# Values and keys turned block-wise on VectorE and placed by GpSimd; 86 dense steps ahead of the corner; the inverses' round trip on GpSimd's queue

## The chip, the cores and the metric

The kernel runs on one core of a Trainium2 chip. The metric is the device time of one execution in microseconds (us). Engines are named as in the profile: PE (TensorE matmul), PEld (its weight loads), DVE (VectorE), ACT (ScalarE), POOL (GpSimd), SP (SyncE, which issues most DMAs).

## What is computed

One layer of a bidirectional mixer on 384 tokens (128 of context, 256 latent). A combined projection `h @ w_in` feeds a gated short convolution and an RWKV-7 scan with 32 heads of 64 channels, run forwards and backwards:

```python
def step(S, inp):
    r_t, w_t, k_t, v_t, a_t, b_t = inp
    sa = jnp.einsum('dbhij,dbhj->dbhi', S, a_t)
    S = S * w_t[..., None, :] + sa[..., :, None] * b_t[..., None, :] + v_t[..., :, None] * k_t[..., None, :]
    y = jnp.einsum('dbhij,dbhj->dbhi', S, r_t)
    return S, y
```

The branches are gated, projected (`w_out_a`, `w_out_b`), merged, projected by `w_o`, added to the input and normalised. The final scan states of the context are outputs too.

## The kernel before

**Dense stream.** All large projections run in fp32 as three matmuls of split operands (`mm3`, lines 81 to 83; `hi*hi`, `hi*lo`, `lo*hi`). The class `Stream` cuts them into steps: one step is three matmuls of 128x384 for one column block and one slice of the contraction. A pair of column blocks is 32 steps. Weights are loaded by SP (`raw`), split by ACT (`whi`, line 88) and DVE (`wlo`, line 89) four slices at a time. Pairs have tags: `rk` (r and k of a block), `gv` (gate of a block and v of the next), `bc`, `bx`, `bg`, `gb` (convolution branch), `ma`, `mb` (merge gates), `ob`, and last `oa`, which needs the finished branch A.

**Blocks.** The scan is done in 16 blocks of two heads (`b`), in chunks of 64 tokens (6 chunks, 2 directions). The loop at lines 961 to 990 writes dense steps between the pieces of a block's work, so PE's order is the order of the code. PE's order is fixed by hand; the order on DVE, ACT, POOL and SP is set by a scheduler from the same code. Per block:

- `prep_b`: the products `bk` (keys, 128 channels x 6 chunks x 128) and `pr`, 14 dense steps, then the triangular matrices `A` (PE line 703, masked by DVE line 709, direction by direction with 6 dense steps behind each). POOL scales `bk` by the chunk's decay (line 716). The diagonal 32x32 blocks of `A` go by DMA through DRAM (`ui`) into `U` (48 matrices, one per partition), DVE inverts them in 60 dependent instructions (lines 724 and 726), and the inverses go back by DMA (`uo`, line 729) into `A` (line 734). DVE then turns two of them into `x11` (line 737).
- `prep_c`: states are loaded; PE transposes v (`pv`, 6 transposes, into `sav`) and the scaled `bk` (`pb`, 10 transposes, into `bt`), ACT copies them out of PSUM.
- `prep_a` of the next block, once its `gv` pair is done, and dense steps until `WINDOW` = 80 of them have passed since `prep_b` (104 in block 0 with `FIRST`, 96 in block 15 with `LAST`).
- the corner in `scan`: `pav` (line 850, needs `sav`), `pH` (line 842, needs `x11`), `pX`, then two chains of `po`, `pq`, `pu` with dense steps between; POOL clears part of `A` (line 863).
- `norm`, and in the next block `finish`, which stores the block's part of branch A in DRAM (`ya_d`). After block 15 the rest of `ob` runs, `load_ya` loads all 16 parts back through three buffers (`yst_a`), and `oa` starts.

Of the kernel before, what the change touches and what calls it, by code (L numbers as in the profile page):

```python
# [21 lines left out]
C = 64  # L22
NCH = 6
# [33 lines left out]
def hybrid_step(ctx, tc, cst, x_prompt, x_sample, state_f, state_b, c, c_ctx, ada_w, ada_b, norm_g,  # L57
                w_in, mu_prev, mu_next, w0, w2, a0, a2, k_k, k_a, r_k, lnx_g, lnx_b, conv_w,
                w_out_a, w_out_b, w_o, final_g, y_prompt, y_sample, ns_f, ns_b):
    nc = tc.nc  # L60
# [30 lines left out]


    PB0, PB1, H0, H1, CH0, CH1 = 14, 6, 3, 4, 2, 4
    PRO, WINDOW, FIRST, LAST = 32, 80, 24, 16

    def wload(view, k0, cols, nm):

# [84 lines left out]
    ds_ = Stream()  # L182
# [226 lines left out]
    def tmp(nm):  # L409
        return box["sp"].tile([P, T], F32, tag="t", name=nm, bufs=8)  # L410
# [179 lines left out]
    def bank(nm):  # L590
        return ps1.tile([P, 4, P], F32, tag="A", name=nm, bufs=5)
# [4 lines left out]
    def flat(a):  # L596
        return a.rearrange("p n t -> p (n t)")
# [44 lines left out]
    def prep_k(b, o):  # L642
# [6 lines left out]
        for d in range(2):  # L649
# [14 lines left out]
            o["kd"].append(kd)  # L664
            o["bn"].append(aa)

    def prep_b(b, o):

        r, kk = r_[b], o["kk"]
# [27 lines left out]
        for d in range(2):  # L697
            pr, bk = o["pr"][d], o["bk"][d]
            m0 = C_MB if d else C_MF
            pas = {(h, n0): bank(f"pA_{b}_{d}_{h}_{n0}") for n0 in (0, 4) for h in range(2)}  # L700
            for n in range(NCH):
                for h in range(2):
                    TE.matmul(pas[h, n // 4 * 4][:, n % 4, :], bk[hss[h], n, :], pr[hss[h], n, :],  # L703
                              start=True, stop=True)
            for n0, w in ((0, 4), (4, 2)):
                mk = cs[:, m0:m0 + P].rearrange("p (w t) -> p w t", t=C).unsqueeze(1).broadcast_to([P, w, 2, C])
                for h in range(2):
                    f0 = NCH * d + n0
                    V.tensor_tensor(A[:, :, f0:f0 + w, hss[h]].rearrange("p w n t -> p n w t"),
                                    pas[h, n0][:, 0:w, :].rearrange("p n (w t) -> p n w t", t=C), mk, ALU.mult)  # L710
            yield PB1
            for e in range(2):
                nc.sync.dma_start(ui[d, e].rearrange("i s t -> s i t"), blocks(A, d, e))

        for d in range(2):
            G.tensor_tensor(o["bk"][d][:], o["bk"][d][:], o["ep"][d][:, :, C:C + 1].broadcast_to([P, NCH, P]), ALU.mult)

        U = sp.tile([48, 32, 32], F32, tag="U", name=f"U_{b}")
        nc.sync.dma_start(U[:], ui[:].rearrange("d e i s t -> (d e i) s t"))
# [6 lines left out]
            V.tensor_tensor(U[:, 0:s, s + 1:], U[:, 0:s, s + 1:], tv, ALU.add)  # L726
        dg = U[:].rearrange("p a b -> p (a b)")[:, 0:1024:33]
        V.tensor_scalar(dg, dg, 1.0, None, ALU.add)
        nc.sync.dma_start(uo[:].rearrange("d e i s t -> (d e i) s t"), U[:])
        x11 = sp.tile([64, 24, 32], F32, tag="x11", name=f"x11_{b}")  # L730
        o["x11"] = x11
        for e in range(2):
            for d in range(2):
                nc.sync.dma_start(blocks(A, d, e), uo[d, e].rearrange("i s t -> s i t"))

        for d in range(2):
            box["turned"] = V.transpose(x11[0:32, 12 * d:12 * d + 12, :], blocks(A, d, 0)).ins

    def prep_c(b, o):

        r, v, A = r_[b], v_[b], o["A"]

        s_in = sp.tile([P, 2, C], F32, tag="s_in", name=f"s_in_{b}")
        for d in range(2):
            for h in range(2):
                for jb in range(2):
                    p0 = C * h + 32 * jb
                    nc.sync.dma_start(s_in[p0:p0 + 32, d, :].rearrange("i (b j) -> i b j", j=32),
                                      ctx_st[d][0, 0, 2 * b + h].rearrange("(b i) j -> i b j", i=32)
                                      [:, :, 32 * jb:32 * jb + 32])  # L750

        sav = sp.tile([P, 2 * NCH, P], F32, tag="sav", name=f"sav_{b}")
        bt = sp.tile([P, 2 * NCH, P], F32, tag="bt", name=f"bt_{b}")
        o["sav"], o["bkt"] = sav, bt
        for d in range(2):
            if d == 0:
                src = v
            else:
                src = tmp(f"vr_{b}")
                S.copy(src[:], v[:, ::-1])  # L760
            pv = bank(f"pv_{b}_{d}")
            for q in range(3):
                TE.transpose(pv[:, q, :], src[:, q * P:(q + 1) * P], ident)
            for e in range(2):
                S.copy(sav[C:P, NCH * d + e:NCH * d + NCH:2, :], pv[C * e:C * e + C, 0:3, :])
            yield 1
        for d in range(2):

            for n0, n1 in (((0, 4), (4, 5)), ((0, 3), (4, 6)))[d]:
                pb = bank(f"pb_{b}_{d}_{n0}")  # L770
                for n in range(n0, n1):
                    TE.transpose(pb[:, n - n0, :], o["bk"][d][:, n, :], ident)
# [167 lines left out]
        V.tensor_tensor(ya[:], ya[:], ga_[b][:], ALU.mult)  # L940
        nc.sync.dma_start(ya_d[b], ya[:])

    def drive(gen, prio=0, at=None, fn=None):
        n = i = 0
        while True:
            if i == at:
                fn()
            i += 1
            with tc.high_priority(offset=prio):
                u = next(gen, None)  # L950
            if u is None:
                return n
            ds_.go(u)
            n += u
# [2 lines left out]
    cur = {}  # L957
    drive(prep_a(0, cur))
    prep_k(0, cur)
    prev = None  # L960
    for b in range(NB):
        if b < NB - 1:
            if b > 0:
                ds_.urgent += [(add_rk, b + 1), (add_gv, b)]
        if b == NB - 2:
            ds_.fills += [(add_gv, NB - 1)] + [(add_ob, g) for g in range(8)]
        pb_gen = prep_b(b, cur)
        ds_.go(next(pb_gen))
# [203 lines left out]
```

## Time and profile before

| | |
|---|---|
| runs | 2235.28, 2237.07, 2239.02 us (median 2237.07) |
| the profiled execution | 2234.36 us, span 2232.6 us |
| granted TensorE clock | 0.998 |
| PE, PEld, DVE, ACT, POOL busy | 2173.1, 2062.7, 1553.3, 1013.5, 115.7 us |
| DVE inversion, lines 724 and 726, 960 instructions | 309.3 us |
| POOL, line 716, 32 instructions | 49.3 us |
| ACT, copies out of `pv` and `pb`, lines 765 and 773 | 55.4 us |

PE is busy nearly throughout, so the time is PE's work plus the moments when its next instruction waits. Busy shares of the others matter only where such a wait ends on them. A matmul's recorded duration overlaps with the next one's; what it costs is read from the distance of the starts.

### The profile page before, as it was taken

What the parts mean: (1) busy time and instruction counts of PE and PEld (TensorE: products, weight loads), DVE (VectorE), ACT (ScalarE), POOL (GpSimd) and SP (SyncE); (2) the same over time, 40 slices, a digit from 0 to 9 for tenths busy, and PEclk for the clock granted to TensorE, in tenths of its full rate; (3) what the DMA queues carried; (4) which work ended last, traced back from release to release, by engine and by line L of the source; (5) the groups of instructions that cost most, each with busy time, mean ns of one, the idle gap of its engine ahead of it and who ended that gap; (6) DMA issues with size and microseconds to landing.
All of it is one profiled execution on the core that took longest, in us unless ns stands there. A gap on an engine that the chain in (4) does not pass through costs nothing.

```text
span 2232.6 us, 40518 instructions
## 1 busy us (share of the span) xinstructions
PE 2173.1 (97%) x16020; PEld 2062.7 (92%) x16020; DVE 1553.3 (70%) x3240; ACT 1013.5 (45%) x1784; POOL 115.7 (5%) x113
## 2 busy tenths in 40 slices
PE   5999999999999999999999999999999999999998
PEld 3589999999999999999999999999999999998988
DVE  3259567787878878777878787887777785444354
ACT  4245435454545454444445454546454633333333
POOL 2000000000000000000000000000000000000000
PEclk9999999999999999999999999999999999999999
DMA  9974454444343435343444434344445464886633
GB/s 338 346 211 128 131 141 116 116 117 118 108 132 107 130 100 131 106 130 100 121 108 127 112 107 133 107 122 126 124 118 139 144 196 143 294 281 233 220 132 113
DMA packets 426574, 335.25 MB, mean 150 GB/s; under 512 B 82496, under 2 KB 408720, under 8 KB 425488
## 3 DMA queue, kind: packets, MB, share of 16 engines
q1 hardware_dynamic: 424896, 330.91, 50.2%
q8 instruction: 126, 2.06, 0.4%
q10 hardware_dynamic: 432, 1.57, 0.2%
q14 instruction: 64, 0.52, 0.1%
q0 software_dynamic: 1056, 0.19, 0.1%
HBM read 305.80 MB, written 26.21 MB: 149 GB/s over the span
## 4 chain that ended last, share of the span: by engine, by line
PE 74%; DVE 12%; DMA 6%; ACT 4%; issue 2%; SPq 1%; POOL 0%; POOLq 0%; DVEq 0%; ACTq 0%
DMA raw_adah<-in_ada_w_dram 4%; PE d_rk L81 3%; PE d_rk L82 3%; PE d_rk L83 3%; PE d_gv L81 3%; PE d_gv L82 3%; PE d_gv L83 3%; PE d_oa L81 2%; PE pA L703 2%; PE d_oa L83 2%; PE d_oa L82 2%; PE d_mb L81 2%; PE d_mb L83 2%; PE d_mb L82 2%; PE d_bc L81 2%
## 5 line engine op out<-in xcount | busy, mean ns | idle before, releaser
L724 DVE TENSOR_TENSOR ut<-U 48x30 f32<-48x30 f32 (+14 forms) x480 | 154.8, 323 | 18.3 <-DMA U<-ui 5.5
L81 PE MATMUL d_rk<-h_hi,whi_rk 128*128 128x384 f32 x480 | 161.7, 337 | 0.6 <-ACT lst L554 0.6
L726 DVE TENSOR_TENSOR U<-U,ut 48x30 f32<-48x30 f32 (+14 forms) x480 | 154.5, 322 | 11.1
L81 PE MATMUL d_gv<-h_hi,whi_gv 128*128 128x384 f32 x480 | 160.6, 335 | 0.0
L82 PE MATMUL d_rk<-h_lo,whi_rk 128*128 128x384 f32 x480 | 160.5, 334 | 0.0
L83 PE MATMUL d_rk<-h_hi,wlo_rk 128*128 128x384 f32 x480 | 160.4, 334 | 0.0
L83 PE MATMUL d_gv<-h_hi,wlo_gv 128*128 128x384 f32 x480 | 160.4, 334 | 0.0
L82 PE MATMUL d_gv<-h_lo,whi_gv 128*128 128x384 f32 x480 | 160.4, 334 | 0.0
L88 ACT CAST whi_gv<-raw_gv 128x1024 fp32r<-128x1024 f32 (+1 forms) x64 | 64.0, 999 | 139.6 <-PE d_rk L82 100.0
L88 ACT CAST whi_rk<-raw_rk 128x1024 fp32r<-128x1024 f32 x60 | 63.0, 1054 | 110.8 <-PE d_rk L82 34.7
L89 DVE TENSOR_TENSOR wlo_rk<-raw_rk,whi_rk 128x1024 fp32r<-128x1024 f32 x60 | 72.9, 1218 | 45.3 <-ACT whi_rk L88 35.6
L81 PE MATMUL d_bc<-h_hi,whi_bc 128*128 128x384 f32 x256 | 92.2, 360 | 0.0
L81 PE MATMUL d_gb<-h_hi,whi_gb 128*128 128x384 f32 x256 | 92.2, 360 | 0.0
L81 PE MATMUL d_bg<-h_hi,whi_bg 128*128 128x384 f32 x256 | 92.2, 360 | 0.0
L81 PE MATMUL d_bx<-h_hi,whi_bx 128*128 128x384 f32 x256 | 92.1, 360 | 0.0
L81 PE MATMUL d_ma<-h_hi,whi_ma 128*128 128x384 f32 x256 | 91.6, 358 | 0.0
L81 PEld LDWEIGHTS d_rk<-h_hi,whi_rk 128*128 128x128 f32 x480 | 90.1, 188 | 0.9 <-ACT lst L554 0.9
L81 PE MATMUL d_mb<-h_hi,whi_mb 128*128 128x384 f32 x256 | 90.4, 353 | 0.0
L81 PEld LDWEIGHTS d_gv<-h_hi,whi_gv 128*128 128x128 f32 x480 | 90.1, 188 | 0.2
L81 PE MATMUL d_ob<-ybh,whi_ob 128*128 128x384 f32 x256 | 88.4, 345 | 2.0 <-DVE smb L521 1.0
L82 PEld LDWEIGHTS d_rk<-h_lo,whi_rk 128*128 128x128 f32 x480 | 90.2, 188 | 0.0
L82 PEld LDWEIGHTS d_gv<-h_lo,whi_gv 128*128 128x128 f32 x480 | 90.1, 188 | 0.0
(315 smaller groups left out, 6548.4 us busy)
## 6 DMA issues: line engine op xcount, KB each, us to landing
raw_adah<-in_ada_w_dram SPq DMA_DIRECT2D x64, 512.0 KB, 8.7
raw_rk<-in_w_in_dram SPq DMA_DIRECT2D x60, 512.0 KB, 5.3
raw_gv<-in_w_in_dram SPq DMA_DIRECT2D x60, 512.0 KB, 4.9
raw_ma<-in_w_in_dram SPq DMA_DIRECT2D x16, 1024.0 KB, 5.6
raw_mb<-in_w_in_dram SPq DMA_DIRECT2D x16, 1024.0 KB, 5.6
raw_bc<-in_w_in_dram SPq DMA_DIRECT2D x16, 1024.0 KB, 5.5
raw_bx<-in_w_in_dram SPq DMA_DIRECT2D x16, 1024.0 KB, 5.4
raw_bg<-in_w_in_dram SPq DMA_DIRECT2D x16, 1024.0 KB, 5.5
```

Of the source, the lines that this page charges most:

```text
L81: TE.matmul(out, wh, xh, start=start, stop=False)
L82: TE.matmul(out, wh, xl, start=False, stop=False)
L83: TE.matmul(out, wl, xh, start=False, stop=stop)
L88: S.copy(hi[0:rows], src)
L89: V.tensor_tensor(lo[0:rows], src, hi[0:rows].bitcast(F32), ALU.subtract)
L703: TE.matmul(pas[h, n // 4 * 4][:, n % 4, :], bk[hss[h], n, :], pr[hss[h], n, :], start=True, stop=True)
L724: V.tensor_tensor(tv, U[:, 0:s, s:s + 1].broadcast_to([48, s, w]), U[:, s:s + 1, s + 1:].broadcast_to([48, s, w]), ALU.mult)
L726: V.tensor_tensor(U[:, 0:s, s + 1:], U[:, 0:s, s + 1:], tv, ALU.add)
```

## The change

The 16 PE transposes of a block and their eight ACT copies are gone, and so is ACT's reversed copy of v. DVE turns `bk` in place in 32x32 blocks (two instructions of 128x768 a block) and v (two of 128x384, in the scan of the block before), and POOL moves the 32x32 blocks to their places: 32 copies into `bt`, 16 into `sav`, each of 32 partitions x 192. The store `uo` and the four loads into `A` are issued by POOL. `WINDOW` is 86, `FIRST` 18, `LAST` 10, so blocks 0 and 15 keep 104 and 96 steps; `prep_a` starts exactly 12 steps ahead of the corner.

```diff
-    PRO, WINDOW, FIRST, LAST = 32, 80, 24, 16
+    PRO, WINDOW, FIRST, LAST, PA = 32, 86, 18, 10, 12
...
+    def prep_v(b, o):
+        o["vt"] = []
+        for d in range(2):
+            x = sp.tile([P, T], F32, tag=f"vt{d}", name=f"vt_{b}_{d}")
+            V.transpose(x[:], v_[b][:, ::-1] if d else v_[b][:])
+            o["vt"].append(x)
...
+        with tc.issue_after(last):
+            for d in range(2):
+                V.transpose(flat(o["bk"][d][:]), flat(o["bk"][d][:]))
+        bt = sp.tile([P, 2 * NCH, P], F32, tag="bt", name=f"bt_{b}")
+        with tc.issue_after(lam):
+            for d, p, q in ((d, p, q) for d in range(2) for p in range(4) for q in range(4)):
+                put = G.tensor_copy(bt[32 * p:32 * p + 32, NCH * d:NCH * d + NCH, 32 * q:32 * q + 32],
+                                    o["bk"][d][32 * q:32 * q + 32, :, 32 * p:32 * p + 32]).ins
+        sav = sp.tile([P, 2 * NCH, P], F32, tag="sav", name=f"sav_{b}")
+        with tc.issue_after(put):
+            for d in range(2):
+                x = o["vt"][d][:].rearrange("p (n e t) -> p n e t", e=2, t=32)
+                for e in range(2):
+                    for q in range(4):
+                        G.tensor_copy(sav[C + 32 * e:C + 32 * e + 32, NCH * d:NCH * d + NCH, 32 * q:32 * q + 32],
+                                      x[32 * q:32 * q + 32, :, e, :])
...
-        nc.sync.dma_start(uo[:].rearrange("d e i s t -> (d e i) s t"), U[:])
+        G.dma_start(uo[:].rearrange("d e i s t -> (d e i) s t"), U[:])
...
-                nc.sync.dma_start(blocks(A, d, e), uo[d, e].rearrange("i s t -> s i t"))
+                G.dma_start(blocks(A, d, e), uo[d, e].rearrange("i s t -> s i t"))
...
-            pv = bank(f"pv_{b}_{d}")
-            for q in range(3):
-                TE.transpose(pv[:, q, :], src[:, q * P:(q + 1) * P], ident)
-            for e in range(2):
-                S.copy(sav[C:P, NCH * d + e:NCH * d + NCH:2, :], pv[C * e:C * e + C, 0:3, :])
-            yield 1
...
-                pb = bank(f"pb_{b}_{d}_{n0}")
-                for n in range(n0, n1):
-                    TE.transpose(pb[:, n - n0, :], o["bk"][d][:, n, :], ident)
-                S.copy(bt[:, NCH * d + n0:NCH * d + n1, :], pb[:, 0:n1 - n0, :])
-                yield 1
...
+        w = WINDOW + (FIRST if b == 0 else LAST if b == NB - 1 else 0)
         if b < NB - 1:
-            while f"gv{b}" not in ds_.done:
+            while n < w - PA or f"rk{b + 1}" not in ds_.done:
                 ds_.go(1)
                 n += 1
             n += drive(prep_a(b + 1, nxt))
```

What stands on POOL in block 7, before: the last instruction of block 6 (the root in `norm`), the scaling of `bk`, the clearing of `A`, the root of block 7. The trailing numbers of the names only tell buffers apart.

```order
L929 TENSOR_TENSOR rs_9588<-var_9585,nhalf 128x6
L716 TENSOR_TENSOR bk_0_9592<-bk_0_9592,ep_1152 128x768
L716 TENSOR_TENSOR bk_1_9598<-bk_1_9598,ep_1154 128x768
L863 MEMSET A_9656 64x1536
L929 TENSOR_TENSOR rs_10736<-var_10733,nhalf 128x6
```

and after, from the scaling on:

```order
L725 TENSOR_TENSOR bk_0_9808<-bk_0_9808,ep_1152 128x768
L725 TENSOR_TENSOR bk_1_9814<-bk_1_9814,ep_1154 128x768
L734 COPY bt_9973<-bk_0_9808 32x6x32 x16
L734 COPY bt_9973<-bk_1_9814 32x6x32 x16
L743 COPY sav_10006<-vt_0_9493 32x6x32 x8
L743 COPY sav_10006<-vt_1_9495 32x6x32 x8
L758 DMA uo_9873<-U_10023 48x1024
L763 DMA A_9874<-uo_9873 32x12x32 x4
L868 MEMSET A_9874 64x1536
L934 TENSOR_TENSOR rs_10989<-var_10986,nhalf 128x6
```

So 48 copies and five DMA issues came between the scaling and the clearing of `A`, and the store of the inverses stands behind the copies.

What stands on DVE in block 7 from the last masked piece of `A` into the inversion, before:

```order
L709 TENSOR_TENSOR A_9656<-pA_1_1_4_9711,cs 128x2x2x64
L89 TENSOR_TENSOR wlo_rk_0_1_9688<-raw_rk_0_9680,whi_rk_0_1_9687 128x1024
L89 TENSOR_TENSOR wlo_rk_1_0_9890<-raw_rk_1_9886,whi_rk_1_0_9889 128x1024
L724 TENSOR_TENSOR ut_9752<-U_9750 48x30
L726 TENSOR_TENSOR U_9750<-U_9750,ut_9752 48x30
L724 TENSOR_TENSOR ut_9752<-U_9750 48x58
```

and after, up to the same point and then a later piece of the same inversion:

```order
L730 STREAM_TRANSPOSE bk_0_9808<-bk_0_9808 128x768
L730 STREAM_TRANSPOSE bk_1_9814<-bk_1_9814 128x768
L89 TENSOR_TENSOR wlo_bx_1_1_9909<-raw_bx_1_9902,whi_bx_1_1_9908 128x1024
L89 TENSOR_TENSOR wlo_rk_0_0_10133<-raw_rk_0_10129,whi_rk_0_0_10132 128x1024
L753 TENSOR_TENSOR ut_10025<-U_10023 48x30
L755 TENSOR_TENSOR U_10023<-U_10023,ut_10025 48x30
```

```order
L755 TENSOR_TENSOR U_10023<-U_10023,ut_10025 48x6x25
L473 SCALAR_TENSOR_TENSOR bu_0_10177<-bc_0_9852,par,bu_0_10177 128x127
L473 SCALAR_TENSOR_TENSOR bu_0_10177<-bc_0_9852,par,bu_0_10177 128x4x63
L475 SCALAR_TENSOR_TENSOR bu_0_10177<-bc_0_9852,par,bu_0_10177 128x127
L475 SCALAR_TENSOR_TENSOR bu_0_10177<-bc_0_9852,par,bu_0_10177 128x4x63
L753 TENSOR_TENSOR ut_10025<-U_10023 48x168
L467 TENSOR_TENSOR bc_1_9898<-bc_1_9898,d_bx_1_9901 128x384
```

Two turns of `bk` stand ahead of the inversion, and in this block the convolution's instructions (lines 467 to 475) moved into it. Before, a block held 160 dense steps (five pairs), and the same pairs fell on the same place in every block; now it holds 165.

PE's own order loses the rows of lines 763 and 772 in every block. Counted in that order, blocks 2 to 14 had 81 dense steps between `prep_b` and the corner and now have 86, block 1 had 95 and now has 86, and after `finish` of block 15 there are 28 dense steps of `ob` left ahead of `oa`, where there were 84.

More of the change, by code (lines that the diff above doesn't have):

```diff
@@ L708, in prep_b @@
                     f0 = NCH * d + n0
-                    V.tensor_tensor(A[:, :, f0:f0 + w, hss[h]].rearrange("p w n t -> p n w t"),
-                                    pas[h, n0][:, 0:w, :].rearrange("p n (w t) -> p n w t", t=C), mk, ALU.mult)
+                    last = V.tensor_tensor(A[:, :, f0:f0 + w, hss[h]].rearrange("p w n t -> p n w t"),
+                                           pas[h, n0][:, 0:w, :].rearrange("p n (w t) -> p n w t", t=C), mk,
+                                           ALU.mult).ins
             yield PB1
@@ L715, in prep_b @@
         for d in range(2):
-            G.tensor_tensor(o["bk"][d][:], o["bk"][d][:], o["ep"][d][:, :, C:C + 1].broadcast_to([P, NCH, P]), ALU.mult)
+            lam = G.tensor_tensor(o["bk"][d][:], o["bk"][d][:],
+                                  o["ep"][d][:, :, C:C + 1].broadcast_to([P, NCH, P]), ALU.mult).ins
+        with tc.issue_after(last):
[14 more added lines that the diff above has]
+                                      x[32 * q:32 * q + 32, :, e, :])
+        o["sav"], o["bkt"] = sav, bt
         U = sp.tile([48, 32, 32], F32, tag="U", name=f"U_{b}")
@@ L739, in prep_c @@
     def prep_c(b, o):
-        r, v, A = r_[b], v_[b], o["A"]
+        r = r_[b]
         s_in = sp.tile([P, 2, C], F32, tag="s_in", name=f"s_in_{b}")
@@ L750, in prep_c @@
                                       [:, :, 32 * jb:32 * jb + 32])
[L752 to L760, printed above, removed]
-            pv = bank(f"pv_{b}_{d}")
-            for q in range(3):
-                TE.transpose(pv[:, q, :], src[:, q * P:(q + 1) * P], ident)
-            for e in range(2):
-                S.copy(sav[C:P, NCH * d + e:NCH * d + NCH:2, :], pv[C * e:C * e + C, 0:3, :])
-            yield 1
-        for d in range(2):
-            for n0, n1 in (((0, 4), (4, 5)), ((0, 3), (4, 6)))[d]:
-                pb = bank(f"pb_{b}_{d}_{n0}")
-                for n in range(n0, n1):
-                    TE.transpose(pb[:, n - n0, :], o["bk"][d][:, n, :], ident)
-                S.copy(bt[:, NCH * d + n0:NCH * d + n1, :], pb[:, 0:n1 - n0, :])
-                yield 1
         ks = o["kd"]
@@ L941, in finish, with drive @@
         nc.sync.dma_start(ya_d[b], ya[:])
-    def drive(gen, prio=0, at=None, fn=None):
+    def drive(gen, prio=0, late=()):
         n = i = 0
+        late = list(late)
         while True:
-            if i == at:
-                fn()
+            for x in [x for x in late if i >= x[0] and x[1] in ds_.done]:
+                x[2]()
+                late.remove(x)
             i += 1
@@ L951, in drive @@
             if u is None:
+                assert not late
                 return n
@@ L959, in hybrid_step @@
     prep_k(0, cur)
+    prep_v(0, cur)
     prev = None
@@ L978, in hybrid_step @@
             n += drive(prep_a(b + 1, nxt))
-        w = WINDOW + (FIRST if b == 0 else LAST if b == NB - 1 else 0)
         if n < w:
@@ L986, in keys, with values @@
                 prep_k(b + 1, nxt)
-        drive(scan(b, cur), 300, 3 if b < NB - 1 else None, keys)
+        def values():
+            with tc.issue_after(cur["turn"][1]):
+                prep_v(b + 1, nxt)
+        drive(scan(b, cur), 300, ((3, f"rk{b + 1}", keys), (3, f"gv{b}", values)) if b < NB - 1 else ())
         norm(b, cur)
```

## Prediction

> **What bounds the kernel.** I read the engines' busy time first, then who waited for whom on PE.
>
> ```profile
> PE 2173.1 (97%) x16020; PEld 2062.7 (92%) x16020; DVE 1553.3 (70%) x3240; ACT 1013.5 (45%) x1784; POOL 115.7 (5%) x113
> ```
> ```profile
> PE pada L292 <- DMA raw_adah<-in_ada_w_dram: 22.4, 16, 9.4
> PE po L804 <- DVE st L833: 7.6, 9, 1.6
> ```
>
> PE is the bound; its largest wait lies in the prologue, the next is 7.6 us in the whole scan. So PE work that goes is worth its time, if nothing arrives later than PE. Next, PE in order of time in block 7, at the transposes, and a stretch of dense steps alone.
>
> ```profile
> 949.04 0.33 PE L81 MATMUL d_bc<-h_hi,whi_bc 128*128 128x384 f32 x1
> ...
> 949.56 0.49 PE L763 MATMUL pv<-cs,v 128*128 128x128 f32 x3
> ...
> 950.42 0.49 PE L763 MATMUL pv<-cs,vr 128*128 128x128 f32 x3
> ...
> 951.27 0.60 PE L772 MATMUL pb<-cs,bk 128*128 128x128 f32 x4
> ...
> 954.48 0.34 PE L81 MATMUL d_rk<-h_hi,whi_rk 128*128 128x384 f32 x1
> ...
> 1063.18 0.33 PE L81 MATMUL d_rk<-h_hi,whi_rk 128*128 128x384 f32 x1
> ...
> 1067.34 0.33 PE L81 MATMUL d_rk<-h_hi,whi_rk 128*128 128x384 f32 x1
> ```
>
> From 1063.18 to 1067.34 are eight steps: 0.52 us each. From 949.04 to 954.48 are seven steps and all 16 transposes: 5.44 - 7 x 0.52 = 1.80 us for the transposes.
>
> Third, the path that has to arrive at the corner in time, in block 7 (DVE, SP and PE in order of time), then the turn of the inverses and `pH` in blocks 1, 2, 14 and 15.
>
> ```profile
> 945.98 1.95 DVE L709 TENSOR_TENSOR A<-pA,cs 128x512 f32<-128x512 f32 x4 [0.66 <-PE pA L703]
> 954.87 1.23 DVE L89 TENSOR_TENSOR wlo_rk<-raw_rk,whi_rk 128x1024 fp32r<-128x1024 f32 x1 [4.48 <-ACT whi_rk L88]
> 956.05 0.18 DVE L724 TENSOR_TENSOR ut<-U 48x30 f32<-48x30 f32 x1
> 985.11 0.21 DVE L726 TENSOR_TENSOR U<-U,ut 48x30 f32<-48x30 f32 x1
> 985.34 0.34 SPq L729 DMA_DIRECT2D uo<-U  x1
> 988.01 1.99 SPq L734 DMA_DIRECT2D A<-uo  x4
> 992.87 1.17 DVE L737 STREAM_TRANSPOSE x<-A 32x384 f32<-32x384 f32 x2 [1.16 <-DMA A<-uo]
> 997.70 0.62 PE L842 MATMUL pH<-x,A 32*32 32x32 f32 x48
> ```
> ```profile
> 357.62 1.22 DVE L737 STREAM_TRANSPOSE x<-A 32x384 f32<-32x384 f32 x2 [0.98 <-DMA A<-uo]
> 367.88 0.62 PE L842 MATMUL pH<-x,A 32*32 32x32 f32 x48
> 470.16 1.19 DVE L737 STREAM_TRANSPOSE x<-A 32x384 f32<-32x384 f32 x2 [0.71 <-DMA A<-uo]
> 472.29 0.62 PE L842 MATMUL pH<-x,A 32*32 32x32 f32 x48
> 1726.86 1.03 DVE L737 STREAM_TRANSPOSE x<-A 32x384 f32<-32x384 f32 x2 [1.20 <-DMA A<-uo]
> 1731.65 0.62 PE L842 MATMUL pH<-x,A 32*32 32x32 f32 x48
> 1844.73 0.56 DVE L737 STREAM_TRANSPOSE x<-A 32x384 f32<-32x384 f32 x1
> 1845.68 0.62 PE L842 MATMUL pH<-x,A 32*32 32x32 f32 x48
> ```
>
> The chain is: mask done 947.93, out and back by DMA, inversion 956.05 to 985.32, out and back again 7.55 us, turned 994.04, used 997.70. The margin is 3.7 us here, 9.0 in block 1, 0.9 in block 2, 3.8 in block 14, 0.4 in block 15; over blocks 2 to 14, thirteen such pairs of which the first and the last stand here, it runs from about nothing to 3.8, mean 1.75. So the corner is nearly a second bound: what makes this chain later by more than two microseconds is paid in every block.
>
> **The change part by part.**
>
> *PE work removed.* 1.80 us x 16 = 28.8 us off the path. ACT loses eight copies a block; at 45% busy and with no PE wait on it worth naming, that is worth nothing.
>
> *The window.* Blocks 2 to 14 get five more dense steps ahead of the corner (86 against 81) and lose the transposes there: 5 x 0.52 - 1.80 = +0.8 us for the chain. The steps are only moved, at no PE cost until the supply ends (below). Block 1 goes from 95 to 86 steps, which with the transposes takes 6.5 of its margin of 9.0; block 15 loses 1.8 of its 0.4.
>
> *DVE ahead of the inversion.* Two turns of `bk`, 768 columns where line 737 turns 384 in 0.558 (below), so about 1.0 each, fall where DVE sat idle 4.48 us before 954.87. Nothing, while that idle time holds them.
>
> *DVE inside the inversion.* With 165 steps a block the dense stream's instructions fall differently. Summed over blocks 2 to 14 in DVE's order, the inversion takes in seven more weight splits (1.22), twenty more `scalar_tensor_tensor` (0.41) and twenty more 128x384 instructions (0.55): 27.7 us, 2.1 a block, from 1.5 less in block 10 to 7 more in block 7. In block 7 before, such a sum gives 30.0 for a measured 29.3, and I scale by that.
>
> ```profile
> L422 DVE SCALAR_TENSOR_TENSOR v<-zs,par,v 128x255 f32<-128x255 f32 x16 | 7.6, 476 | 0.0
> L737 DVE STREAM_TRANSPOSE x<-A 32x384 f32<-32x384 f32 x32 | 17.4, 558 | 25.3 <-DMA A<-uo 25.1
> L716 POOL TENSOR_TENSOR bk<-bk,ep 128x768 f32<-128x768 f32 x32 | 49.3, 1541 | 155.6 <-PE pA L703 140.9 <-DMA ui<-A 10.1 <-issue 4.6
> L584 POOL MEMSET ep<- 128x390 f32 x4 | 1.5, 426 | 0.0
> L579 POOL MEMSET st<- 128x256 f32 x2 | 0.6, 312 | 38.8 <-PE pe L83 38.8
> ```
>
> *POOL's copies, by themselves.* The trace has no copy on POOL. Its memsets cost 0.85 ns an element and 0.09 fixed, so 0.26 us for 192; its two-operand product gives 0.39 to 0.46. A copy reads one operand, so I take 0.30, near the memset: 14 us for 48. They start at the first turned `bk`, about a microsecond after the mask, and the corner is 48 us further on; `uo` behind them is due 37 us after the mask. Time enough.
>
> *POOL's copies against DVE.* Two places where a reading POOL instruction overlaps a DVE instruction with two operands in SBUF:
>
> ```profile
> 304.59 1.49 POOL L716 TENSOR_TENSOR bk<-bk,ep 128x768 f32<-128x768 f32 x1 [5.21 <-PE pA L703]
> 305.22 1.27 DVE L940 TENSOR_TENSOR ya<-ya,ga 128x384 f32<-128x384 f32 x1
> 415.89 0.56 DVE L940 TENSOR_TENSOR ya<-ya,ga 128x384 f32<-128x384 f32 x1
> 416.28 1.51 POOL L716 TENSOR_TENSOR bk<-bk,ep 128x768 f32<-128x768 f32 x1 [4.19 <-PE pA L703]
> ```
>
> At 305.22 DVE needed 1.27 instead of 0.56: it was held until about 305.93, 0.15 before POOL ended. At 416.28 POOL began 0.17 before DVE ended and lost only 0.02. So the two exclude each other, but only up to 0.15 before the end. All 60 steps of the inversion have two such operands. From the first turned `bk` (949) to its start (956) are 7 us, less two weight splits, so about 18 copies fit ahead; 30 fall between its steps. Steps follow each other 0.03 after an end; with a copy between, the next one starts 0.15 before the copy's end, which itself started 0.15 before the last step's end: a delay of c - 0.33. At 0.30 that is nothing, at 0.45 it is 3.6 us a block; weight splits, which follow without a gap, add 0.5. I take 0.5, with 0 and 4 as ends.
>
> *The second round trip on POOL's queue.* POOL now waits there for the last step, then for `uo`; behind that stand only the clearing of `A`, which is due after `pav`, and the root in `norm`. On SP the weight loads no longer stand behind these five, which is worth nothing, since PE's waits name no weight.
>
> ```profile
> A<-uo SPq DMA_DIRECT2D x64, 48.0 KB, 3.6
> m<-in_ada_b_dram POOLq DMA_DIRECT2D x16, 1.0 KB, 5.5
> ```
>
> By SP it takes 7.55 us from issue to turn. POOL's small loads took 5.5 us to land in the crowded prologue; two such hops and a second issue are 11.5, 4 more. On the other side, on a queue of its own the 48 KB loads need not stand behind weight loads: 2 less. I take 0.5 less. [...]
>
> *Stalls at the corner.* Let x be the sum of the last two terms, 0.0 by my values. Each block's own DVE extra, less 0.8, less its own margin, gives stalls in blocks 2, 7, 9 and 13 of 2.4, 2.4, 3.3 and 0.7, and 2.4 in block 15: 11 us together. With x = 2 the same sum is 26, with 4 it is 52, with 5 it is 67, with 9 it is 127.
>
> *The turns of v* (two of 0.56 in the scan) hide in DVE's slack there; PE waits for DVE only 7.6 us in all scans. Without that cover they cost up to 15 us.
>
> *The end.* `finish` of block 15, the first load back of branch A, and its last split:
>
> ```profile
> 1890.64 0.52 PE L936 MATMUL py<-cs,ytok 128*128 128x128 f32 x3 [0.21 <-DVE ytok L930]
> 1897.53 1.27 SPq L507 DMA_DIRECT2D yst_a<-ya_d  x3
> 1928.61 1.21 DVE L509 TENSOR_TENSOR yal<-yst_a,yah 128x384 fp32r<-128x384 f32 x2 [1.10 <-ACT yah L508]
> ```
>
> Before, 84 steps (44 us) of `ob` covered these 39 us. Now 28 steps do, 14.6 us, and `oa` needs its last slice 27 steps, 14 us, later. At the pace seen, PE would wait 10 us in all (39 less 29); without the `ob` weights between the loads perhaps 2. I take 6.
>
> *Sum* against the profiled execution (2234.4): 2234.4 - 28.8 + 11 + 6 = 2222.6. The median of the runs stands 2.7 above that execution, so about 2225.5 on the median.
>
> **Rivals.** *DVE is held longer* (slower): POOL holds DVE for whole copies, or a copy costs nearer 0.45 with a fixed part that also excludes. For it: the overlaps show a hold; against it: the 0.15 us at each end. Thirty copies at 0.30 give x = 9; I price it at x = 5: 2234.4 - 28.8 + 67 + 6 = 2279, 2281 on the median. It decides from x = 1.8, where stalls eat the 28.8 - 6. [...]
>
> *The inverses come back later by POOL's queue* (slower): 3 us more, x = 3, stalls 39, 2250.6, median 2253. For it: 5.5 us at POOL; against it: that was the prologue, beside the heaviest loads.
>
> *The gain is eaten* (within 0.2%, 4.5 us, about what a measurement of this kernel can tell from no change): x between 1.2 and 2.2, or 1 with the end at 10 us. Median 2237.
>
> **How the numbers follow.** Forecast 0.48, with its own range 2209 (no stalls, the end at 2) to 2232; DVE held 0.25; later inverses 0.13; eaten 0.14. Faster is the forecast; slower is the sum of the two, 0.38. Predicted 2226. For 8 in 10 the range leaves a tenth out at each side: 2210 to 2285, the upper end just past the first rival's price.
>
> **What would show it.** PE's rows of the transposes gone and 16 x 1.8 us of it; POOL's copies at 0.3 or not; the inversion's first to last step at 29 to 31 us on average (35 and more: DVE is held); from the last step to the turn 7 to 8 us (10 and more: POOL's queue); `pH` waiting in blocks 7 and 9 but not in 10; a wait of PE at the first steps of `oa`, none there before. I am wrong if the copies, spread over partitions, cost twice the memset, or if weight splits held up on DVE make dense steps wait.

## The result, and the profile after

The changed kernel takes 2298.95 us (median of 4 runs, 2295.28 to 2301.20) against 2237.74: ratio 1.0273, 95% interval 1.0256 to 1.0291. It is 61 us slower, above the top of the predicted range (2285). The profiled execution took 2301.20 us, with a span of 2299.4 against 2232.6 before. First PE's busy time from the page of the changed kernel, then who waited for whom on PE (microseconds in all, times, longest).

```profile
PE 2177.8 (95%) x15764; PEld 2060.4 (90%) x15764; DVE 1637.3 (71%) x3304; ACT 938.7 (41%) x1627; POOL 609.6 (27%) x961
```
```profile
PE pl L83 <- DVE lwl L89: 13.2, 6, 3.8
PE pH L847 <- DVE x L766: 13.0, 10, 2.7
PE d_ob L81 <- ACT ybh L508: 6.9, 2, 6.7
PE d_bg L81 <- DVE ga L440: 6.0, 2, 4.7
PE d_gb L81 <- DVE ga L440: 4.4, 2, 2.3
PE d_oa L81 <- ACT yah L508: 4.0, 3, 2.9
PE d_oa L82 <- DVE yal L509: 3.7, 5, 0.9
PE d_bc L81 <- DVE bg L486: 3.4, 1, 3.4
PE d_ob L82 <- DVE ybl L509: 2.7, 2, 2.3
```

PE has 256 instructions fewer, the transposes, yet is busy 4.7 us longer. Without 28.8 us of transposes (the prediction's price) it should be busy 2144.3, so the same work takes 33.5 more. And it is idle 2299.4 - 2177.8 = 121.6 us where it was idle 59.5: 62.1 more. 33.5 + 62.1 - 28.8 = 66.8, the difference of the spans.

**The idle time** is not mainly at the corner. `pH` has 13 us; as much goes to `pl`, the LoRA matmuls of `prep_a`, waiting for the split of their weights; 18 us (with smaller rows not shown) to dense steps that wait until VectorE has emptied a PSUM buffer (`ga`, `bg` are the instructions that read it); 9.6 to the first steps of `ob` and 7.7 to those of `oa`. Before, the dense steps inside the blocks waited 0.6 us in all, and `pl` this:

```profile
PE pl L83 <- DVE lwl L89: 1.7, 1, 1.7
```

**The longer busy time** is, for the most part, a lower clock. One such wait, in block 6: PE in order of time, then windows with the granted clock (the number ahead of the DMA share).

```profile
893.41 0.34 PE L83 MATMUL d_bg<-h_hi,wlo_bg 128*128 128x384 f32 x1
898.42 0.69 PE L81 MATMUL d_bg<-h_hi,whi_bg 128*128 128x384 f32 x1 [4.67 <-DVE ga L440]
898.91 0.52 PE L82 MATMUL d_bg<-h_lo,whi_bg 128*128 128x384 f32 x1
899.23 0.52 PE L83 MATMUL d_bg<-h_hi,wlo_bg 128*128 128x384 f32 x1
```
```profile
896.00:898.00 2.00, 0.00 (x0) 0.00 (x0) 1.86 (x6) 0.00 (x0) 0.03 (x1) 0.95 0.37 71
898.00:900.00 2.00, 1.57 (x5) 1.58 (x6) 1.97 (x4) 0.00 (x0) 0.00 (x0) 0.50 1.08 381
902.00:904.00 2.00, 2.00 (x7) 2.00 (x7) 1.98 (x6) 1.04 (x1) 0.00 (x0) 0.50 0.00 0
906.00:908.00 2.00, 2.00 (x14) 2.00 (x13) 1.15 (x7) 0.33 (x1) 0.42 (x1) 1.00 0.88 282
```

After a wait of 4.67 us the matmuls start 0.32 apart in place of 0.173, until about 905, at a granted clock of 0.50. Cut into windows of 1 us, busy time times (1 - granted clock) sums to 31.0 us over this execution and to 1.7 before: 29.3 of the 33.5. The 62.1 us of added idle time brought 29.3 of low clock, so a wait was paid about one and a half times. With the low clock's share taken off, PE is busy 2171.4 us before and 2146.7 here: 24.7 less, where the transposes were priced at 28.8. In the other runs without transposes and with the copies on GpSimd or left out, the same sum gives 2145.5 to 2149.2. So the price of the transposes is about right, perhaps a few us too high.

**VectorE and GpSimd.** Groups (busy us, mean ns, idle before): the two lines of the inversion in the kernel before; then, in the changed kernel, the copies on GpSimd and the same two lines; then three instructions of block 6 in order of time.

```profile
L724 DVE TENSOR_TENSOR ut<-U 48x30 f32<-48x30 f32 (+14 forms) x480 | 154.8, 323 | 18.3 <-DMA U<-ui 5.5
L726 DVE TENSOR_TENSOR U<-U,ut 48x30 f32<-48x30 f32 (+14 forms) x480 | 154.5, 322 | 11.1
```
```profile
L734 POOL COPY bt<-bk 32x192 f32<-32x192 f32 x512 | 262.4, 513 | 42.2 <-DVE bk L730 21.6
L753 DVE TENSOR_TENSOR ut<-U 48x30 f32<-48x30 f32 (+14 forms) x480 | 175.7, 366 | 28.7 <-DMA U<-ui 17.6
L755 DVE TENSOR_TENSOR U<-U,ut 48x30 f32<-48x30 f32 (+14 forms) x480 | 174.9, 364 | 11.5
L743 POOL COPY sav<-vt 32x192 f32<-32x192 f32 x256 | 177.0, 692 | 11.5
```
```profile
888.96 0.43 DVE L755 TENSOR_TENSOR U<-U,ut 48x238 f32<-48x238 f32 x1
889.20 0.41 POOL L743 COPY sav<-vt 32x192 f32<-32x192 f32 x1
889.42 0.43 DVE L753 TENSOR_TENSOR ut<-U 48x240 f32<-48x240 f32 x1
```

A step of the inversion takes 0.365 on average (0.322 before). The mean of a copy, 0.51 or 0.69, is that of two kinds. 647 of the 768 copies took under 1 us, 0.35 on average into `bt` and 0.43 into `sav`; beside the inversion they run in step, one copy to one step, 0.46 from one to the next in these rows. The other 121 took 1.2 us and more, up to 5.99. Each of them lies beside a run of VectorE instructions (weight splits, the shifts of r and k, steps between them) in which each starts before the one ahead has ended, and all 121 end 0.20 to 0.22 us behind the end of one of these instructions. From first to last step the inversion takes 34.6 us on average over blocks 2 to 14 (30.3 before).

### The profile page after: what moved, and what is told of

The parts are those of the page before. It is cut to its first block, busy times and chain, and to the rows that moved or that the text cites. A ratio compares the mean times of both kernels' runs of the same rounds, so it can differ in the third digit from the quotient of the medians.

```text
span 2299.4 us, 40645 instructions
## 1 busy us (share of the span) xinstructions
PE 2177.8 (95%) x15764; PEld 2060.4 (90%) x15764; DVE 1637.3 (71%) x3304; ACT 938.7 (41%) x1627; POOL 609.6 (27%) x961
## 5 line engine op out<-in xcount | busy, mean ns | idle before, releaser
L734 POOL COPY bt<-bk 32x192 f32<-32x192 f32 x512 | 262.4, 513 | 42.2 <-DVE bk L730 21.6
L934 POOL TENSOR_TENSOR rs<-var,nhalf 128x6 f32<-128x6 f32 x16 | 22.9, 1432 | 717.2 <-DVE var L932 717.2
L753 DVE TENSOR_TENSOR ut<-U 48x30 f32<-48x30 f32 (+14 forms) x480 | 175.7, 366 | 28.7 <-DMA U<-ui 17.6
L755 DVE TENSOR_TENSOR U<-U,ut 48x30 f32<-48x30 f32 (+14 forms) x480 | 174.9, 364 | 11.5
L743 POOL COPY sav<-vt 32x192 f32<-32x192 f32 x256 | 177.0, 692 | 11.5
L725 POOL TENSOR_TENSOR bk<-bk,ep 128x768 f32<-128x768 f32 x32 | 53.1, 1661 | 151.2 <-PE pA L711 137.5
L81 PE MATMUL d_oa<-yah,whi_oa 128*128 128x384 f32 x256 | 87.8, 343 | 4.1 <-ACT yah L508 4.0
```

The source lines that it names most:

```text
L81: TE.matmul(out, wh, xh, start=start, stop=False)
L725: lam = G.tensor_tensor(o["bk"][d][:], o["bk"][d][:], o["ep"][d][:, :, C:C + 1].broadcast_to([P, NCH, P]), ALU.mult).ins
L734: put = G.tensor_copy(bt[32 * p:32 * p + 32, NCH * d:NCH * d + NCH, 32 * q:32 * q + 32], o["bk"][d][32 * q:32 * q + 32, :, 32 * p:32 * p + ...
L743: G.tensor_copy(sav[C + 32 * e:C + 32 * e + 32, NCH * d:NCH * d + NCH, 32 * q:32 * q + 32], x[32 * q:32 * q + 32, :, e, :])
L753: V.tensor_tensor(tv, U[:, 0:s, s:s + 1].broadcast_to([48, s, w]), U[:, s:s + 1, s + 1:].broadcast_to([48, s, w]), ALU.mult)
L934: G.tensor_tensor(rs[:], var[:], nhalf[:], ALU.pow)
```

## Experiments: the parts one by one

Theory A: the copies slow VectorE, and what VectorE does for PE comes late. Theory B: the places (86 steps, `prep_a` 12 ahead of the corner). Theory C: the turns on VectorE. Besides these, GpSimd's queue. Ratios are to the kernel before; a difference of ratios is taken times 2237 us.

**The queue.**
```diff
-        G.dma_start(uo[:].rearrange("d e i s t -> (d e i) s t"), U[:])
+        nc.sync.dma_start(uo[:].rearrange("d e i s t -> (d e i) s t"), U[:])
...
-                G.dma_start(blocks(A, d, e), uo[d, e].rearrange("i s t -> s i t"))
+                nc.sync.dma_start(blocks(A, d, e), uo[d, e].rearrange("i s t -> s i t"))
```


> The changed kernel with the store of the inverses and the four loads issued by SP as before. If GpSimd's queue made the second round trip late: from the last step of the inversion to the turn 1 us less, and 5 to 20 us off. By theories A, B and C: within 5 us of the changed kernel, 2294 to 2304; the trace of the changed kernel has 8.3 us there on average against 7.9.

Measured 2271.52, ratio 1.0153 (1.0138 to 1.0168): the queue costs 27 us, more than any theory had. Block 7, the store, the loads and the turn in the changed kernel, then with SP's queue:

```profile
1019.11 0.60 POOL L758 DMA_DIRECT2D uo<-U  x1 [9.31 <-DVE U L755]
1022.27 2.46 POOL L763 DMA_DIRECT2D A<-uo  x4 [2.56 <-DMA uo<-U]
1027.28 1.03 DVE L766 STREAM_TRANSPOSE x<-A 32x384 f32<-32x384 f32 x2 [6.20 <-DMA A<-uo]
1027.99 0.91 PE L847 MATMUL pH<-x,A 32*32 32x32 f32 x48 [2.35 <-DVE x L766]
```
```profile
1016.26 0.34 SPq L758 DMA_DIRECT2D uo<-U  x1
1020.71 0.57 DVE L766 STREAM_TRANSPOSE x<-A 32x384 f32<-32x384 f32 x1 [2.54 <-DMA A<-uo]
```

From the store to the turn are 8.2 us against 4.5 here; over blocks 2 to 14 the means are 8.05 and 6.21. The kernel before needed 8.1 with SP, so the comparison with it hid the price: in the new places SP's trip is shorter, 6.45 in the run of the places alone below. With SP, `pH` no longer waits, `pl` waits 8.8, and of the 33.5 us that PE was busy longer 21 are left.

**The places alone.** The kernel before with only the constants and the place of `prep_a`:
```diff
-    PRO, WINDOW, FIRST, LAST = 32, 80, 24, 16
+    PRO, WINDOW, FIRST, LAST, PA = 32, 86, 18, 10, 12
...
-            while f"gv{b}" not in ds_.done:
+            while n < w - PA or f"rk{b + 1}" not in ds_.done:
```


> The kernel before with only the constants 86, 18, 10 and prep_a 12 steps ahead of the corner; transposes on PE, ACT copies, SP's queue as before. Theory A: no copies on GpSimd, so VectorE is not late, 2232 to 2245. Theory B: the same waits of pl for lwl and of d_ steps for ga appear here, 2260 or more.

2264.73, ratio 1.0121 (1.0104 to 1.0138): 27 us lost with no copy and no turn. But not by theory B's waits; `pl` waits 3.4 us. PE's waits of this run:

```profile
PE d_ob L81 <- ACT ybh L508: 6.9, 1, 6.9
PE d_oa L81 <- ACT yah L508: 4.3, 3, 3.6
PE d_oa L82 <- DVE yal L509: 3.5, 4, 0.9
PE d_ob L82 <- DVE ybl L509: 2.9, 2, 2.0
```

These are the two places where the dense stream changes its operand. With 165 steps a block `ob` starts in the scan of block 14, beside the preparation of block 15; before, its first steps lay among the matrices of block 15. The operand takes the place of `h` and comes through buffers that this preparation uses too. SP issued its first load at 1787.25, 4.7 us after the start of the last matmul that reads `h`; until then it had waited for VectorE and ACT to be done with such a buffer (SP's waits from 1783 to 1787.5):

```profile
SPq L507 <- DVE L L654: 3.3, 1, 3.3
SPq L507 <- ACT sig L657: 0.9, 1, 0.9
```

That `ob` follows right behind that last step isn't enough for a wait: in the best version below it does so too, with the loads issued 8 us ahead, and waits for nothing there. And `oa` starts behind 28 steps of cover. Besides, PE is busy 11.4 us longer, of which the low clock is 8.1.

**The changed kernel in the old places** (80, 24, 16, `prep_a` behind the gate pair):
```diff
-    PRO, WINDOW, FIRST, LAST, PA = 32, 86, 18, 10, 12
+    PRO, WINDOW, FIRST, LAST, PA = 32, 80, 24, 16, 12
...
-            while n < w - PA or f"rk{b + 1}" not in ds_.done:
+            while f"gv{b}" not in ds_.done:
```


> The changed kernel with the constants and the place of prep_a as before: 80 steps (24 and 16 more in the first and last block), prep_a as soon as the block's gate pair is done. The turns, the copies on GpSimd and the queue stay. Theory A (copies slow VectorE): the corner comes 6 steps (3.1 us) earlier and the inversion is as long, so the corner waits more, 2300 to 2340. Theory B (places): the waits of pl for lwl (13 us) and of the d_ steps for ga (17 us) go, and the low clock behind them; 2240 to 2265.

2322.99, ratio 1.0384: as theory A had it. The corner, 3.1 us earlier, now waits far more. So the new places, which cost 27 us alone, save 24 beside the copies and GpSimd's queue: the parts don't simply add.

```profile
PE pH L847 <- DVE x L766: 47.9, 19, 6.3
PE pl L83 <- DVE lwl L89: 22.3, 15, 3.5
```

**Without the copies.**
```diff
-                put = G.tensor_copy(bt[32 * p:32 * p + 32, ...], o["bk"][d][...]).ins
+            put = G.memset(bt[:], 0.0).ins
...
-                        G.tensor_copy(sav[C + 32 * e:C + 32 * e + 32, ...], x[...])
+            G.memset(sav[C:P, :, :], 0.0)
```


> The changed kernel with its 48 copies a block left out: bt and the lower half of sav are filled with zeros by one GpSimd memset each (write only), so the turned keys and values are not used in the result. The turns on VectorE, the places and GpSimd's queue stay. Theory A (the copies slow VectorE, and VectorE's lateness is what PE waits for): the inversion's instructions back at 0.32 us, pl's wait for lwl and the d_ steps' wait for ga and bg nearly gone, the corner's wait gone, the low clock behind them too; what is left is the added cost of the new places (27 us measured alone) less the transposes (29): 2235 to 2250. Theory C (the turns): 2275 or more.

2257.91, ratio 1.0098 (1.0083 to 1.0113): the copies cost 39 us; the time is above theory A's range and below theory C's. The steps of the inversion are as fast as before, and it takes 31.85 us from first to last, where it took 34.6; the trip from the store to the turn stays at 8.1, so the copies don't act through GpSimd's queue. The waits of the dense steps for VectorE fall from 18 to 7.7 us, those of `pl` to 6.5, those of `pH` to 3.2.

```profile
L748 DVE TENSOR_TENSOR U<-U,ut 48x30 f32<-48x30 f32 (+14 forms) x480 | 154.1, 321 | 11.3
L746 DVE TENSOR_TENSOR ut<-U 48x30 f32<-48x30 f32 (+14 forms) x480 | 154.0, 321 | 29.2 <-DMA U<-ui 18.3
```

**Without the turns** (the copies read unturned tiles):
```diff
-                V.transpose(flat(o["bk"][d][:]), flat(o["bk"][d][:]))
...
-            V.transpose(x[:], v_[b][:, ::-1] if d else v_[b][:])
-            o["vt"].append(x)
+            o["vt"].append(v_[b])
```


> The changed kernel with the four turns of a block (bk and v, 48 us of VectorE in all) left out: the 48 copies read the unturned tiles, so bt and sav hold blocks that are not turned. Theory C (the turns make VectorE late): most of the waits go, 2240 to 2260. Theory A (the copies): the inversion's instructions stay at 0.36 us, 2280 to 2300.

2292.82, ratio 1.0244 (1.0227 to 1.0261): 6 us less, with intervals that overlap, for 45 us less work on VectorE. Theory C falls.

**The copies on ScalarE:**
```diff
-                put = G.tensor_copy(bt[32 * p:32 * p + 32, ...], o["bk"][d][...]).ins
+                put = S.copy(bt[32 * p:32 * p + 32, ...], o["bk"][d][...]).ins
...
-                        G.tensor_copy(sav[C + 32 * e:C + 32 * e + 32, ...], x[...])
+                        S.copy(sav[C + 32 * e:C + 32 * e + 32, ...], x[...])
```


> The 48 block copies of a block (bt and sav) are issued on ScalarE in place of GpSimd; all else is as in the changed kernel. Theory A (the copies on GpSimd slow VectorE: the inversion's 960 instructions took 350.6 us against 309.3, and what stands between them on VectorE comes late): the inversion's instructions fall back to about 0.32 us each, most of PE's 59 us of added waits and the low clock behind them go, 2215 to 2240. Theory B (the places: 86 steps and prep_a 12 steps ahead of the corner put the LoRA weight split and the emptying of PSUM behind the inversion on VectorE): nothing much moves, 2285 to 2300. Theory C (the turns on VectorE, 48 us more of its work): also 2280 to 2300. ScalarE gets about 48 x 0.4 = 19 us a block, at 41% busy; if that delays its own drains, PE waits for ACT instead.

2362.85, ratio 1.0562: a miss. The inversion's steps are at 0.322, as theory A had it, but 48 copies at 0.35 us on ScalarE stand ahead of its own drains and splits, and PE waits for those:

```profile
PE d_gv L81 <- ACT r L418: 18.0, 4, 6.7
PE d_gv L81 <- ACT whi_gv L88: 13.0, 6, 4.4
```

So this run says nothing on the time that the copies cost.

## Experiments: can the gain be had?

**The values alone**, the kernel before with v turned and copied:
```diff
+            V.transpose(x[:], v_[b][:, ::-1] if d else v_[b][:])
...
+                    put = G.tensor_copy(sav[C + 32 * e:C + 32 * e + 32, ...], x[...]).ins
...
-                TE.transpose(pv[:, q, :], src[:, q * P:(q + 1) * P], ident)
```


> The kernel before, and of the change only the values: v turned by VectorE in the scan, 16 copies a block on GpSimd at the block's start; the keys are still transposed on PE, with 80 steps and SP's queue. 6 of 16 transposes go: 16 x 1.80 x 6/16 = 10.8 us off PE. Theory A: the 16 copies (5.4 us) end ahead of the inversion, so nothing on VectorE is held there; 2226 to 2232. If the turns of v in the scan (18 us of VectorE) are what makes VectorE late: 2240 or more.

2260.45, ratio 1.0104, and not for either reason given. The copies stood on GpSimd ahead of the root `rs`, so the norm, and PE in `finish`, waited for them:

```profile
PE py L939 <- DVE ytok L933: 20.6, 16, 1.7
```

**The same with the copies behind the root:**
```diff
+        box["rs"] = G.tensor_tensor(rs[:], var[:], nhalf[:], ALU.pow).ins
...
+        with tc.issue_after(box["rs"]) if "rs" in box else ExitStack():
             ... the 16 copies into sav
```


> As the run with the values alone, but the 16 copies of v stand on GpSimd behind the root in norm and not ahead of it. There PE waited 20.6 us for ytok in finish, since the root (and with it ytok) came behind the copies. If that is all that was wrong with it: 2226 to 2234. If the copies or the turns of v cost by themselves: 2245 to 2260.

2237.67, ratio 1.0001 (0.9991 to 1.0010), between the two ranges. The wait is gone, but the 10.8 us are not gained. The dense steps, which waited 0.6 us in the blocks before, wait for VectorE (8.5 us in these rows), and 6.5 us are lost at the low clock against 1.7. Whether the turns of v or their copies make VectorE late here wasn't taken apart.

```profile
PE d_gb L81 <- DVE bu L480: 3.2, 3, 1.1
PE d_bg L81 <- DVE bc L467: 3.2, 3, 1.1
PE d_bc L81 <- DVE bg L486: 2.1, 2, 1.1
```

**Copies of the keys held until the inversion ends**, SP's queue:
```diff
+        put = G.tensor_copy(gate_[:], U[:, 0, 0:1]).ins
+        with tc.issue_after(put):
             ... the 32 copies into bt
```


> The changed kernel with SP's queue for the inverses, the 16 copies of v at the start of the block and the 32 copies of the keys held until the inversion's last step by one small GpSimd copy that reads U. Theory A: the inversion's instructions at 0.32 us, waits of pl and of the d_ steps back to a few us, 2235 to 2250; the 32 copies take 11 us by themselves and are due when pu of the first chain starts, about 12 us behind, so a wait of pu for bt of up to 2 us a block would add up to 30. If only the queue mattered: as SP's queue alone, 2271.

2280.90, ratio 1.0198, a miss. The inversion's steps are at 0.329, but here too the copies of v stood ahead of the root, and `py` waited 21.6 us for `ytok`.

**Steps moved from ahead of the matrices to behind them**, in the kernel before (14 to 8, 80 to 86; a block keeps 160 steps, so `ob` and `oa` start as before):
```diff
-    PB0, PB1, H0, H1, CH0, CH1 = 14, 6, 3, 4, 2, 4
+    PB0, PB1, H0, H1, CH0, CH1 = 8, 6, 3, 4, 2, 4
-    PRO, WINDOW, FIRST, LAST = 32, 80, 24, 16
+    PRO, WINDOW, FIRST, LAST = 32, 86, 18, 10
...
+        drive(pb_gen)
         if prev is not None:
             finish(b - 1, prev)
-        drive(pb_gen)
```


> The kernel before, with 6 of the 14 dense steps ahead of the triangular matrices moved behind them (14 to 8, 80 to 86, 24 to 18, 16 to 10) and finish of the block before issued behind the matrices; a block keeps its 160 steps. If the 27 us of the new places alone come from where the two changes of operand (the start of ob, the start of oa) fall, and not from the longer window: no loss here, 2230 to 2240. If the longer window itself costs: 2250 or more.

2246.58, ratio 1.0042 (1.0026 to 1.0059), between the two ranges. `ob` and `oa` cost little; among PE's waits that grew, the largest are 6.7 us of `pv` waiting for ACT's reversed v, and 4.6 in block 0. So most of the 27 us isn't the longer window's: this run, with the same window, loses 9.

**All of it together.** To the run with the keys' copies held are added the copies of v behind the root, the moved steps with `finish` behind the matrices as in the run just above, and `prep_a` behind the gate pair again:
```diff
+        with tc.issue_after(box["rs"]) if "rs" in box else ExitStack():
             ... the 16 copies into sav
...
-    PB0, PB1, H0, H1, CH0, CH1 = 14, 6, 3, 4, 2, 4
+    PB0, PB1, H0, H1, CH0, CH1 = 8, 6, 3, 4, 2, 4
...
-            while n < w - PA or f"rk{b + 1}" not in ds_.done:
+            while f"gv{b}" not in ds_.done:
```


> A version put together from the findings: no transposes on PE, the turns on VectorE, the copies of v on GpSimd behind the root in norm, the copies of the keys held until the inversion's last step, SP's queue for the inverses, and 86 steps behind the matrices with 8 instead of 14 ahead of them, so that a block keeps 160 steps; prep_a as soon as the gate pair is done. If the copies, the queue and the places are what cost: 2237 less 29, and up to 15 for what is left of waits, 2208 to 2225. If the turns on VectorE or the low clock after short waits still take it back: 2235 or more.

2243.38, ratio 1.0023 (1.0014 to 1.0032), as the second branch had it. All transposes are gone, and yet nothing is gained: `pl` waits 12.8 us for `lwl`, the dense steps some 15 for VectorE, and 10.3 are lost at the low clock.

**A fourth PSUM buffer for the dense steps**, one less for the scan, in the changed kernel, in the kernel before, and in the combined version, which also gets the last line:
```diff
-    pd = ctx.enter_context(tc.tile_pool(name="pd", bufs=3, ...))
+    pd = ctx.enter_context(tc.tile_pool(name="pd", bufs=4, ...))
...
-        return ps1.tile([P, 4, P], F32, tag="A", name=nm, bufs=5)
+        return ps1.tile([P, 4, P], F32, tag="A", name=nm, bufs=4)
...
-        yield PB0
+        yield PB0 if b else 14
```


> The changed kernel with four PSUM buffers for the dense steps in place of three, and four in place of five for the scan. If the d_ steps' waits for VectorE (17 us and some of the low clock behind them) are a cost of their own: they go, 2275 to 2288. If they only move to the next wait on the late VectorE: 2292 or more. If four buffers are too few for the scan: slower than 2299, with waits of pA or pH for a buffer.

2304.14, ratio 1.0301 (1.0286 to 1.0316), no better than without it. The waits of dense steps for `ga` are gone, and VectorE's lateness shows at its next readers:

```profile
PE pl L83 <- DVE lwl L89: 20.1, 8, 7.1
PE pH L847 <- DVE x L766: 17.8, 12, 3.4
```

A smaller part is the scan's lost buffer: `pH` also waits 2.9 us until ACT has read `pl`, which shares these buffers (0.7 in the changed kernel).

> The kernel before with the same four and four buffers, as a control: it had no wait of d_ steps worth naming in the blocks, so 2234 to 2241. If the scan needs its fifth buffer: 2245 or more.

2242.18, ratio 1.0019 (1.0009 to 1.0030), between the two ranges: the buffer brings the kernel before nothing, rather a little loss.

> The combined version with the four and four buffers, and 14 steps ahead of the matrices again in block 0 alone. Its d_ steps waited about 13 us for VectorE; without these and the 3 us of block 0: 2222 to 2230. If VectorE's lateness only shows elsewhere: 2238 or more.

2217.44, ratio 0.9910 (0.9895 to 0.9924): 20 us faster than the kernel before, the best version here and better than expected. PE's busy time is 7.7 above 2144.3, with 6.5 us lost at the low clock, and of the waits on VectorE little is left:

```profile
PE 2152.0 (97%) x15764; PEld 2041.3 (92%) x15764; DVE 1613.9 (73%) x3304; ACT 952.2 (43%) x1640; POOL 475.1 (21%) x897
```
```profile
PE po L811 <- DVE st L840: 6.3, 12, 1.6
PE pq L828 <- POOL A L870: 5.1, 4, 1.9
PE pl L83 <- DVE lwl L89: 2.4, 4, 1.7
```

The wait of `pl` went with those of the dense steps (12.8 to 2.4), which I had not expected. Of the 26 us against the run before it, about 3 belong to block 0 (`pA`'s wait there falls from 4.2 to 0.9), the rest goes with the buffer. `pq` now waits for GpSimd's clearing of `A`, which in the trace stands behind the held copies of the keys.

**Two more steps of time for the LoRA split:**
```diff
                 lwh, lwl = split(lraw[:], [96, 2, P], "lwh", "lwl", ...)
-                yield 2
+                yield 4
...
             sig.append(t)
-            yield 2
+            yield 1
```


> As the combined version with four and four buffers, and in prep_a four steps instead of two between the LoRA split and the matmuls that read it (one instead of two behind each of the four matmuls). pl's wait for lwl (12.8 us over ten blocks) goes: 2210 to 2220. If VectorE is the bound there, the wait moves to its next reader: within 3 us of z_banks.

2223.00, ratio 0.9940 (0.9923 to 0.9957), outside both ranges: no gain, 6 us worse; `pl` still waits 6.1, spread over nine places.

## Why the prediction was wrong

Taken out of the changed kernel one at a time, the queue costs 27 us, the copies 39, the turns 6 (within the noise); put alone into the kernel before, the places cost 27. With the transposes at the prediction's -28.8, which no run takes out alone, that is +70 where +61 was measured. The parts aren't independent, so this is no exact account: without the queue's change or without the copies, most of the 13 us at `pH` go either way (none left, 3.2 left), and the places, which cost 27 alone, save 24 beside the others. No run takes out the queue and the copies together and leaves the rest.

*The steps that failed:*

- **The window** ("only moved, at no PE cost until the supply ends"): 0 was put, 27 measured. The 6 us for the end of `ob`'s supply were about right in idle time (7.7 at `oa`), but the start of `ob` was overlooked (9.6 us), whose loads must wait for the buffers of block 15's preparation, and so was the low clock behind both.
- **POOL's copies against DVE** ("I take 0.5"): 2.75 us a block, 34.6 less 31.85, inside the ends of 0 and 4. The price of a copy was nearly right, 0.34 (most copies that nothing held) for 0.30. What was wrong is the picture of a copy that slips into the gap ahead of the next step for nothing: copy and step run in step with each other, and the steps take longer by it, 48x30 from 0.19 to 0.25 and 48x238 from 0.40 to 0.45 on average. Over 60 steps, 0.043 each gives 2.6 of the 2.75.
- **The second round trip** ("I take 0.5 less"): 1.84 more than SP in the same places (8.05 against 6.21). The forecast compared with the kernel before, where SP took 8.1; in the new places SP's trip is shorter as well. Why it is was not tested.
- **A wait costs its length.** This was never put as a step, and every stall in the sum rests on it. 29.3 us more at the low clock stand behind 62 us of added waiting, and the sum had no such term. The stalls of the sum were 3.3 us at most, and the low clock stood behind shorter waits too, one of 2.37 us and one of 1.08 (last section).
- **Where a late VectorE shows.** The stalls were summed at the corner alone: 11 us, and `pH` did wait 13. That agreement is luck: with the 2.75 of the copies the sum's own table gives over 26 there, and of the five blocks with a forecast stall (2, 7, 9, 13, 15) three waited, while 1, 4, 8 and 11 waited unforeseen. Block 2, for one, did not wait at `pH` (472.83), but `pl` had waited 2.37 us just ahead of it (466.39). And 30 us went to readers of VectorE that the sum did not have, `pl` and the emptying of PSUM. The last sentence of the prediction named late weight splits, which is near to it, without a price.

*The rivals.* VectorE was held longer and the inverses came back later, at 39 and 27 us where these rivals were priced at 55 and 27 above the forecast. That the second number agrees is luck: it was priced at 3 us a block, all of it stalls at the corner, while 1.84 were measured, and of what SP's queue wins back 13 are at the corner, 4.4 at `pl` and 12.4 in PE's busy time. The two were weighed as alternatives, but both came at once, with the places and the clock beside them; the range ended just past the price of one.

*What was right:* the transposes' price, roughly; `pH` waiting in blocks 7 and 9 and not in 10; the wait at `oa`; v's turns hiding in the scan (`po` waits 5.7 us, and 6.1 without the turns). Nothing for ACT's copies may be right; no run tests it. Two of the tests were set badly: from the last step to the turn 8.3 us were measured, between 7 to 8 ("right") and 10 ("POOL's queue"), while the queue did cost 27; and the inversion at 34.6 was under the 35 that should show a held VectorE. Both tests compared with the kernel before and not with the same places. A small slip: 2222.6 and 2.7 make 2225.3, not 2225.5.

## What to carry to other kernels

When an engine beside the bound gets more work, list everything that the bound engine reads from it, buffers that it must empty included, and price the lateness at each; cover against it (here a fourth PSUM buffer) paid only once the lateness was small: 5 us lost in the changed kernel, where the intervals overlap, and over 20 won in the combined version. Price a move of steps by what falls at the places where the stream changes its operand. And several parts that can all cost can do so at once: the range has to hold that case, too.

## What the hardware showed that I had not expected

In the changed kernel the low clock, a granted 0.50, came in whole pieces of 3.4 us: the 13 stretches up to 2011 us are 3.4, 6.8, 10.2 or 13.6 us long. I estimate a piece of 3.4 at 0.50 to cost up to 1.7 (3.4 x 0.50).

The 13 stretches also start on one fixed grid of 3.413 us: from 34.23 to 361.91 are 96 such pieces, from there to 467.72 are 31. The length of a wait alone did not tell here whether the clock fell; how much of one piece of the grid it filled told more. A wait of 2.37 us at `pl` lay within one piece (464.31 to 467.72), in which PE was busy 39%, and the clock fell to 0.50 behind it; a wait of 2.27 us before a dense step lay across two (785.16 to 791.99), busy 62 and 71%, and the clock stayed at 1.00.

Where no small matmuls (64x64 or 32x32) stood in the piece, it fell after pieces with PE busy up to 39% and once at 64%, at the start of `oa`, and stayed at all others, 48% and above; in the kernel before no piece between the prologue's start and 2222 us was under 54%, and there was no such stretch until the last 7 us, behind a piece of 44%. With small matmuls in the piece it fell at higher shares, after 46, 48, 54 and 68%. The 68% are at the corner of block 1, with a wait of 1.08 behind the matmuls of `pav`:

```profile
361.25 0.76 PE L847 MATMUL pH<-x,A 32*32 32x32 f32 x48 [1.08 <-DVE x L766]
```
```profile
362.00:364.00 2.00, 2.00 (x8) 2.00 (x7) 2.00 (x6) 0.31 (x1) 0.00 (x0) 0.50 0.00 0
```

VectorE's two-input instructions and GpSimd's copies met in two ways. Where VectorE's instructions follow without a gap, a copy took up to 5.99 us. Beside the dependent steps of the inversion no such hold shows: a step of 48x238 takes 0.40 alone and a copy 0.34, and the two together took 0.46 from one step to the next, not 0.74, while VectorE's steps became 13% longer on average (0.365 for 0.322). Whether the clock's loss could be had back without shortening the waits was not tried.
